# Last and first products by halves of the tokens, and local attention on stacked fp32r halves

## The chip, the cores and the metric

The kernel runs on one core of one Trainium2 chip. The metric is device time in microseconds (us) of one execution; the figure for a kernel is the median of several runs. A profile is of one execution. Engines are written as the profile writes them: PE is TensorE's matmuls, PEld its weight loads, DVE is VectorE, ACT is ScalarE, POOL is GpSimd and SP is SyncE, whose queue issues DMAs in this kernel (SPq).

## The reference

512 tokens of 1024 channels go through a first block and then through two layers of a second one, all in fp32. Cut to what matters:

```python
def first_block(x, mem, ...):
    z = rms_norm(x, norm_mix_g) @ w_in            # gating unit and sparse attention (nsa)
    x = x + mixed @ w_out
    x = x + memory_cross_attention(rms_norm(x, norm_mem_g), mem, ...)
    x = x + square(relu(rms_norm(x, norm_ffn_g) @ w_ff1)) @ w_ff2

def mod_norm(x, m, i, g):
    return rms_norm_2(x, g) * (1 + m[:, 3 * i + 1, None]) + m[:, 3 * i, None]
def ffn_sublayer(x, m, i, g, w1, w2):
    return x + HALF_STEP * m[:, 3 * i + 2, None] * swiglu(mod_norm(x, m, i, g), w1, w2)

for l in range(2):                                # second_block; xc: a context of 256 tokens
    m, mc = silu(c) @ w_mod[l] + b_mod[l], silu(c_ctx) @ w_mod[l] + b_mod[l]
    x, xc = ffn_sublayer(x, m, 0, ...), ffn_sublayer(xc, mc, 0, ...)
    u = mod_norm(x, m, 1, ...) @ w_in[l]          # kc, vc: keys and values of the context
    y = concat(conv_mixer(u), pool_mixer(u), neighbourhood_attention(u, kc, vc, rpb[l])) @ w_out[l]
    x = x + m[:, 5, None] * y                     # l == 0: the context has a mixer of its own and a second ffn
    x = ffn_sublayer(x, m, 2, ...)
return rms_norm_2(x, final_g)
```

In the neighbourhood attention 8 heads of 64 channels attend, in four blocks of 128 query tokens, to a band of 256 local keys (with a bias that also masks) and to 256 context keys.

## The kernel before, in words

Activations lie feature-major: a tile holds 128 channels on the partitions and the tokens along a row, so x is eight tiles of 128x512. To keep fp32 accuracy with the faster fp32r matmuls, every product is three: a weight w is split into wh and wl on arrival (ScalarE casts `whi`, VectorE subtracts for `wlo`, line L348), an activation into h and l, and the kernel adds wh·h, wh·l and wl·h (L377, L378, L380 in `gemm_fm`). Weights come in pieces of up to 1024 columns (`raw`), issued on SP; `get` takes the next piece in a written-out list, splits pieces that come after it, and gives VectorE one *tick*: a share of the products of the modulation (c @ w_mod, lines L582, with the weight tile `wm`).

The order of the work is that of the program: each engine runs its queue in order. Beside the main chain the kernel keeps a queue of other work (`fill`: the context's keys, values, mixer, the mixers' products), from which it takes a piece of some us at marked places.

A feed-forward sublayer goes by groups of hidden tiles (`GROUPS1`, `GROUPS2`): `up` makes a group, `dn` multiplies the group before into x (residual on VectorE). In the third and fourth feed-forward stage the 512 tokens of x and the 256 of the context go together: `gemm_fm` gets two outputs, `mm` of 512 columns and `aux` of 256, and takes them in turn for each k. PSUM has five banks for `mm`.

At a **seam** between two sublayers the last residuals end, the sums of squares go over the partitions by a product with ones (L468), give the reciprocal root (L436, L419), are spread over the partitions (L477), and `norm` makes for each k the h tile on ScalarE (L500) and the l tile on VectorE (L502), after a VectorE product with gain and root (L499). `norm_now` surrounds this with fills; the first two products of the next sublayer run k by k beside the norm (`gemm_fm_pair`, L391 to L408).

Local attention (`attend`) runs units (block j, head) through a pipeline: scores of unit i on PE (plain fp32, L1594 to L1599), bias and row maximum on VectorE (L1600 to L1603), the exponential on ScalarE in two halves (L1604, L1605); two units later four transposes (L1619) and a ScalarE copy (L1621), and two later P·V (L1636). Biases are loaded on SP (L1592) into three buffers. The first layer's stage lies at 1530 to 1660 us, the second's at 3000 to 3120, with other products (`fill`) between the units. The first block's sparse attention (200 to 460 us) is built alike, with transposed tiles copied by ScalarE (L1096) before P·V (L1110); `mem_kv` makes the memory's keys, squares them on ScalarE (L1160) and sums the squares with a product (L1164).

Of the kernel before, what the change touches and what calls it, by code (L numbers as in the profile page):

```python
# [16 lines left out]
T = 512  # L17
# [3 lines left out]
GROUPS2 = [4, 4, 4, 4, 4, 2]  # L21
GROUPS1 = [4] * 8
# [91 lines left out]
def lay_out(i):  # L114
# [44 lines left out]
    for s, j in enumerate((0, 1, 3)):  # L159
        key = np.arange(256) + BAND[j]  # L160
        if j == 1:
            key = np.concatenate([np.arange(256, 320), np.arange(64, 256)])
# [52 lines left out]

class Body:
    def __init__(self, ctx, tc, d, out, pk, at, order):
# [10 lines left out]
        self.used = []  # L228
# [107 lines left out]
    def ensure(self, i):  # L336
        order = self.order
        while len(self.split) <= min(i, len(order) - 1):
# [4 lines left out]
            hi = self.wp.tile([128, 1024], F32R, tag="whi", name="whi")[:, :nk * nc]  # L343
            lo = self.wp.tile([128, 1024], F32R, tag="wlo", name="wlo")[:, :nk * nc]
# [6 lines left out]
    def get(self, key, tick=1, ahead=2):  # L351
        i = len(self.used)
        self.used.append(key)
        if self.order is None:
            _, _, nk, nc = self.pk.pieces[key]
            w = [self.wp.tile([128, 1024], F32R, tag=t, name=t)[:, :nk * nc] for t in ("whi", "wlo")]
# [12 lines left out]
    def gemm_fm(self, outs, w, cols=slice(None), first=True, last=True):  # L369
# [137 lines left out]
    def norm_now(self, ready, *args):  # L507

        self.fill(FILL_A)
        it = self.norm(*args)  # L510
        next(it)
# [3 lines left out]
        if self.order:  # L515
            self.ensure(len(self.used) + 1)
        for _ in it:
            self.fill(FILL_B / 4)
# [103 lines left out]
    def pipeline(self, units, a, b, c, lag=2, lag_c=1, cost=2000):  # L622
# [381 lines left out]
    def nsa(self, qs, kh, kl, v2, gates, kc, vc, st_q, mh, ml):  # L1004
# [9 lines left out]
        P, PT, st = {}, {}, {}  # L1014
# [49 lines left out]
        def a(un):  # L1064
# [16 lines left out]
            nc.vector.tensor_scalar(m, m, r, -1.0, op0=OP.mult, op1=OP.mult)  # L1081
            P[un] = self.t2(w * n)
# [4 lines left out]
        def bb(un):  # L1087
# [8 lines left out]
            nc.scalar.copy(PT[un], t)  # L1096
# [42 lines left out]
        yield from self.pipeline(units, a, bb, cc, 3)  # L1139

    def mem_kv(self, mem, ss):
# [12 lines left out]
        st = self.b1.tile([128, 8], F32, name="mkst")  # L1154
        for h in range(4):
            p = self.mm()[:, :TC]
            self.gemm_fm([(p, hh, hl)], self.get(("mk", h)))
            nc.scalar.copy(self.mk[:, h], p)
            sq = self.t2(TC)
# [664 lines left out]
```

## Time and profile before

| | |
|---|---|
| median of 3 runs | 3551.36 us (3544.3 to 3551.93) |
| the profiled execution | 3549.73 us |
| its span | 3547.0 us |
| mean granted clock of TensorE | 0.979 |
| busy: PE, DVE, ACT, POOL | 97%, 57%, 34%, 3% |

The span is what the profiler saw of the program; the time has some 2.7 us more around it. The granted clock is a mean of two levels: 1 stands for 2.4 GHz, 0.5 for 1.2 GHz.

### The profile page before, as it was taken

To read this page: it belongs to the slowest core of one execution; us is meant where nothing else is said; L and a number is where in the kernel's file an instruction comes from. 1 tells how busy PE (TensorE), PEld (TensorE's weight loads), DVE (VectorE), ACT (ScalarE), POOL (GpSimd) and SP (SyncE) were. 2 spreads that over 40 slices of the span, in tenths; PEclk is the share of its full clock that TensorE was granted. 3 is DMA by queue.
4 is the path that set the end of the run, shared out by engine and by line. 5 is a ranking of instruction groups with operands and counts; after the bars stand their busy time and mean duration, and the time that the engine had idled before them with its cause. 6 is when DMAs were issued, how large, how long until landed. Compare 5 with 4: busy or idle time off the path is not lost.

```text
span 3547.0 us, 48466 instructions
## 1 busy us (share of the span) xinstructions
PE 3437.6 (97%) x18942; PEld 2966.9 (84%) x18942; DVE 2006.4 (57%) x4287; ACT 1209.6 (34%) x2519; POOL 110.8 (3%) x164
## 2 busy tenths in 40 slices
PE   8878999999999999999999999999999999999999
PEld 7868889788888888888888888888888888878887
DVE  5566657656776667655655555464444354554445
ACT  5445535533332223355422222132212134432222
POOL 1000000100000000000000000010000010000000
PEclk9988999999999999999999999999999999999999
DMA  4543334344444443432333333323233223223332
GB/s 168 172 124 118 94 123 142 123 149 143 145 140 143 145 149 120 144 118 88 96 96 93 96 98 91 94 72 95 90 98 95 78 66 117 61 64 106 100 97 78
DMA packets 140788, 392.60 MB, mean 111 GB/s; under 512 B 15632, under 2 KB 26768, under 8 KB 140048
## 3 DMA queue, kind: packets, MB, share of 16 engines
q1 hardware_dynamic: 92176, 301.42, 26.9%
q10 hardware_dynamic: 48384, 88.10, 8.5%
q8 instruction: 148, 2.42, 0.3%
q14 instruction: 80, 0.66, 0.1%
HBM read 387.36 MB, written 2.10 MB: 110 GB/s over the span
## 4 chain that ended last, share of the span: by engine, by line
PE 87%; DVE 6%; ACT 3%; issue 2%; DMA 1%; POOL 0%; SPq 0%; ACTq 0%; POOLq 0%; DVEq 0%
PE mm L377 20%; PE mm L380 20%; PE mm L378 20%; PE aux L377 5%; PE aux L378 5%; PE aux L380 5%; DVE wlo L348 2%; PE aux L1636 2%; PE mm L1619 1%; PE mm L406 1%; PE mm L407 1%; PE mm L408 1%; PE mm L391 1%; PE mm L392 1%; PE mm L396 1%
## 5 line engine op out<-in xcount | busy, mean ns | idle before, releaser
L348 DVE TENSOR_TENSOR wlo<-raw,whi 128x512 fp32r<-128x512 f32 (+1 forms) x1060 | 695.5, 698 | 455.9 <-ACT whi L347 449.3
L377 PE MATMUL mm<-h,whi 128*128 128x512 f32 (+1 forms) x2352 | 905.1, 385 | 11.5 <-ACT whi L347 11.5
L347 ACT CAST whi<-raw 128x512 fp32r<-128x512 f32 (+1 forms) x1060 | 599.4, 616 | 874.3 <-issue 726.5
L380 PE MATMUL mm<-h,wlo 128*128 128x512 f32 (+1 forms) x2352 | 896.8, 381 | 0.4 <-DVE wlo L348 0.4
L378 PE MATMUL mm<-h,whi 128*128 128x512 f32 (+1 forms) x2352 | 895.1, 381 | 0.3 <-DVE h L1002 0.3
L377 PEld LDWEIGHTS mm<-h,whi 128*128 128x128 f32 x2352 | 446.5, 190 | 105.5 <-ACT whi L347 11.7
L380 PEld LDWEIGHTS mm<-h,wlo 128*128 128x128 f32 x2352 | 447.6, 190 | 57.8 <-DVE wlo L348 1.1
L378 PEld LDWEIGHTS mm<-h,whi 128*128 128x128 f32 x2352 | 446.5, 190 | 56.1 <-issue 0.7
L377 PE MATMUL aux<-h,whi 128*128 128x256 f32 x1056 | 305.2, 289 | 3.3 <-DVE xc L1365 1.9
L378 PE MATMUL aux<-h,whi 128*128 128x256 f32 x1056 | 301.2, 285 | 0.5 <-DVE h L502 0.3
L380 PE MATMUL aux<-h,wlo 128*128 128x256 f32 x1056 | 300.2, 284 | 0.0
L377 PE MATMUL mm<-g,whi 128*128 128x512 f32 (+1 forms) x720 | 279.6, 388 | 0.0
L380 PE MATMUL mm<-g,wlo 128*128 128x512 f32 (+1 forms) x720 | 278.8, 387 | 0.0
L378 PE MATMUL mm<-g,whi 128*128 128x512 f32 (+1 forms) x720 | 277.8, 386 | 0.0
L582 DVE CUSTOM_DVE_ANT_0 wm<-wm,silu_c 128x512 f32<-128x512 f32 x336 | 231.2, 690 | 20.0 <-DMA wm<-in_wmod 13.9
L1411 DVE SCALAR_TENSOR_TENSOR t<-t,mm 128x512 f32<-128x512 f32 x88 | 60.5, 687 | 313.4 <-PE mm L380 312.8
L1365 DVE SCALAR_TENSOR_TENSOR x<-mm,gate,x 128x512 f32<-128x512 f32 x160 | 119.9, 749 | 207.2 <-PE mm L380 207.0
L411 ACT CAST g<-t 128x512 fp32r<-128x512 f32 x88 | 54.6, 621 | 526.1 <-DVE t L1411 526.1
L377 PEld LDWEIGHTS aux<-h,whi 128*128 128x128 f32 x1056 | 203.5, 193 | 35.9 <-DVE xc L1365 2.0
L378 PEld LDWEIGHTS aux<-h,whi 128*128 128x128 f32 x1056 | 203.1, 192 | 31.3 <-DVE h L502 1.3
L380 PEld LDWEIGHTS aux<-h,wlo 128*128 128x128 f32 x1056 | 204.5, 194 | 0.0
L377 PEld LDWEIGHTS mm<-g,whi 128*128 128x128 f32 x720 | 135.4, 188 | 28.1
(369 smaller groups left out, 4984.5 us busy)
## 6 DMA issues: line engine op xcount, KB each, us to landing
raw<-in_w_a SPq DMA_DIRECT2D x220, 512.0 KB, 3.5
wm<-in_wmod ACTq DMA_DIRECT2D x336, 256.0 KB, 2.7
raw<-in_w_d SPq DMA_DIRECT2D x110, 512.0 KB, 3.5
raw<-in_w_in SPq DMA_DIRECT2D x84, 512.0 KB, 3.6
raw<-in_w_f SPq DMA_DIRECT2D x64, 512.0 KB, 3.6
raw<-in_w_out SPq DMA_DIRECT2D x32, 512.0 KB, 3.5
bias<-in_bias SPq DMA_DIRECT2D x64, 128.0 KB, 2.2
fc<-in_cw SPq DMA_DIRECT2D x8, 512.0 KB, 4.5
```

Source lines behind the costliest of these rows:

```text
L347: self.nc.scalar.copy(hi[:, cs], raw[:, cs])
L348: self.nc.vector.tensor_tensor(lo[:, cs], raw[:, cs], hi[:, cs].bitcast(F32), op=OP.subtract)
L377: mmul(o, wh[:, k, cols], h[:, k], start=s, stop=False)
L378: mmul(o, wh[:, k, cols], l[:, k], start=False, stop=False)
L380: mmul(o, wl[:, k, cols], h[:, k], start=False, stop=e)
L391: mmul(o, wh[:, k], h[:, k], start=n == 0, stop=False)
L392: mmul(o, wl[:, k], h[:, k], start=False, stop=False)
L411: self.nc.scalar.copy(hi, src)
L582: nc.vector.tensor_tensor_reduce(o, w, self.sc[:, s, ks], 1.0, 0.0, OP.mult, OP.add, wm[:, half, s, j % 8:j % 8 + 1])
L1365: nc.vector.scalar_tensor_tensor(xs, o, gate[:, m:m + 1], xs, op0=OP.mult, op1=OP.add)
L1411: nc.vector.scalar_tensor_tensor(hid, hid, 0.5, b, op0=OP.mult, op1=OP.mult)
L1636: nc.tensor.matmul(o, PT[un][:, k * 128:(k + 1) * 128], v, start=k == 0, stop=k == len(vs) - 1)
```

## The change

`gemm_fm` takes the outputs one after the other. The last `dn` of each sublayer goes by halves of 256 tokens (`tail`), and so do the first two products of the next one (`gemm_halves`); the norm is made per half (`norm_half`), in steps that are issued between these products; `meet` keeps the fills that stood around the norm, ahead of the first products. The last pieces of a feed-forward's second weight are kept in SBUF for both halves (`kept`) and so are all fetched before the first half, in groups `GROUPS1` of 4 and 3 hidden tiles (nine in place of eight) and `GROUPS2` that ends on 3, 3. `mix_out` does its last three tiles by halves. The local attention takes the units by head, then block; scores are four fp32r products over a contraction of 128, made of stacked halves: q1 = [h; l], q2 = [l; h] and kk = [h; l] of one head, built one head ahead (`stack`), q2 by two DMAs from q1. The exponential is one operation of 512 columns and is issued one unit later (`e`); the row maximum is one over 512 columns, the second half of the bias buffer being zero; there are two bias buffers. In the sparse attention the exponential is one step later too, and copies of the first two blocks go to VectorE; in `mem_kv` the sums of squares go one step later.

```diff
-GROUPS2 = [4, 4, 4, 4, 4, 2]
-GROUPS1 = [4] * 8
+GROUPS2 = [4, 4, 4, 4, 3, 3]
+GROUPS1 = [4] * 5 + [3] * 4
+HALVES = (slice(0, 256), slice(256, T))
...
-        for k in range(nk):
-            s, e = first and k == 0, last and k == nk - 1
-            for o, h, l in outs:
+        for o, h, l in outs:
+            for k in range(nk):
+                s, e = first and k == 0, last and k == nk - 1
                 mmul(o, wh[:, k, cols], h[:, k], start=s, stop=False)
                 mmul(o, wh[:, k, cols], l[:, k], start=False, stop=False)
-            for o, h, l in outs:
                 mmul(o, wl[:, k, cols], h[:, k], start=False, stop=e)
...
+    def gemm_halves(self, jobs, hooks={}):
+        mmul = self.nc.tensor.matmul
+        hh, hl = self.h
+        n0, n1 = self.norms
+        for half, cs in enumerate(HALVES):
+            for n in range(9):
+                if half == 0:
+                    n0.to(4 + n)
+                    n1.to({2: 1, 6: 2, 8: 3}.get(n, 0))
+                else:
+                    n1.to(4 + n)
+                    if n in hooks:
+                        hooks[n]()
+                if n < 8:
+                    for o, (wh, wl) in jobs:
+                        mmul(o[:, cs], wh[:, n], hh[:, n, cs], start=n == 0, stop=False)
+                        mmul(o[:, cs], wl[:, n], hh[:, n, cs], start=False, stop=False)
+                if n:
+                    for o, (wh, wl) in jobs:
+                        mmul(o[:, cs], wh[:, n - 1], hl[:, n - 1, cs], start=False, stop=n == 8)
...
+    def norm_half(self, half, ss, g, sh):
+        nc = self.nc
+        cs = HALVES[half]
+        hh, hl = self.h
+        y = self.col_rstd(ss, 256, 1024)
+        yield
+        p = self.spread(y, 2)
+        yield
+        ts = {}
+        for k in range(9):
+            if k < 8:
+                ts[k] = self.t2(256)
+                nc.vector.scalar_tensor_tensor(ts[k], self.x[:, k, cs], g[:, k:k + 1], p[:, :256], op0=OP.mult,
+                                               op1=OP.mult)
+                nc.scalar.activation(hh[:, k, cs], ts[k], AF.Identity, bias=sh[:, k:k + 1])
+            if k:
+                nc.vector.scalar_tensor_tensor(hl[:, k - 1, cs], ts.pop(k - 1), sh[:, k - 1:k],
+                                               hh[:, k - 1, cs].bitcast(F32), op0=OP.add, op1=OP.subtract)
+            yield
...
+    def tail(self, ms, product, residual, ss, l, i, cost, each=None):
+        ss = [Squares(ss.sum[:, cs]) for cs in HALVES]
+        if l < 2:
+            gs, sh = self.mods(l, 0, i)
+            g = self.keep(8)
+            self.nc.vector.tensor_copy(g, gs)
+            self.h = self.new_h()
+            self.norms = [Steps(self.norm_half(h, ss[h], g, sh)) for h in range(2)]
+            steps = {8: (0, 1, 1, 1, 2, 3, 4, 5), 3: (1, 2, 4)}[len(ms)]
+        else:
+            self.ss = ss
+            self.norms = [Steps(self.norm_out())] * 2
+            steps = (0, 0, 1, 1, 1, 1, 2, 2)
+        for h, cs in enumerate(HALVES):
+            late = []
+            for n, m in enumerate(ms):
+                o = self.mm()[:, :256]
+                product(m, o, cs)
+                residual(m, o, cs)
+                self.sq_add(ss[h], self.x[:, m, cs], m, late)
+                if h:
+                    self.norms[0].to(steps[n])
+                if each:
+                    each(h, n)
+                yield cost
...
+            if e is not None and 0 <= i - 1 < n:
+                e(units[i - 1])
...
-            nc.scalar.copy(PT[un], t)
+            if b < 2:
+                nc.vector.tensor_copy(PT[un], t)
+            else:
+                nc.scalar.copy(PT[un], t)
...
+                if g == len(GROUPS1) - 1:
+                    ws = [self.get(("f2", g, m), 1, 3 - m, True) for m in range(4)]
+                    if self.order:
+                        self.ensure(len(self.used) + 1)
+                    def product(m, o, cs):
+                        self.gemm_fm([(o, gh[:, :, cs], gl[:, :, cs])], ws[m // 2], cols=slice(m % 2 * 128, m % 2 * 128 + 128))
+                    return self.run(self.tail(range(8), product, add, self.new_ss(T), 0, 0, 0))
...
+    def stack(self, hd, q_t, k_t):
+        nc = self.nc
+        t, i = hd // 2, hd % 2
+        q1, q2, kk = self.q1[i], self.q2[i], self.kk[i]
+        hs, os = slice(64 * i, 64 * i + 64), slice(64 - 64 * i, 128 - 64 * i)
+        def halves(o, x):
+            nc.scalar.copy(o[hs], x)
+            nc.vector.tensor_tensor(o[os], x, o[hs].bitcast(F32), op=OP.subtract)
+        halves(q1, q_t[hs, t])
+        nc.sync.dma_start(q2[os].bitcast(F32), q1[hs].bitcast(F32))
+        nc.sync.dma_start(q2[hs].bitcast(F32), q1[os].bitcast(F32))
+        yield
+        halves(kk[:, :T], k_t[hs, t])
+        yield
+        halves(kk[:, T:], self.kc[hs, t])
+        yield
+    def attend(self, q_t, k_t, v_t, vc, l, first, mixed, bias, tmp, tmp_t, rows, ready=lambda: True):
+        nc = self.nc
+        units = [(hd, j) for hd in range(8) for j in range(4)]
+        S, P, PT, cur = {}, {}, {}, {}
+        vcf = vc.rearrange("p k n -> p (k n)").rearrange("p (b n) -> p b n", b=2)
+        work = first
+        self.run(work)
+        def a(un):
+            nonlocal work
+            hd, j = un
+            i, b0 = hd % 2, BAND[j]
+            if j == 0 and hd < 7:
+                work = self.stack(hd + 1, q_t, k_t)
+            next(work, None)
+            p = self.mm()
+            if i == 0 and j == 0:
+                cur["s", hd // 2] = self.keep(8)
+            m, pr, bt = self.small(1), tmp(), bias[j % 2]
+            nc.sync.dma_start(bt[:, :256], self.d["bias"][l, (0, 1, 1, 2)[j], hd])
+            for o, ks in ((p[:, :256], slice(b0, b0 + 256)), (p[:, 256:], slice(T, T + TC))):
+                for n, q in enumerate((self.q1[i], self.q2[i])):
+                    nc.tensor.matmul(o, q[:, j * 128:(j + 1) * 128], self.kk[i][:, ks], start=n == 0, stop=n == 1)
+            nc.vector.tensor_tensor_reduce(pr, p, bt, -1.0, 3e38, OP.add, OP.min, m)
+            S[un] = pr, m
...
+        def e(un):
+            hd, j = un
+            n = 4 * (hd % 2) + j
+            P[un], m = S.pop(un)
+            nc.scalar.activation(P[un], P[un], AF.Exp, bias=m, scale=-1.0,
+                                 accum_out=cur["s", hd // 2][:, n:n + 1])
```

How the order of instructions moves at three places. On SP, in the second layer's attention, before (bias<-in_bias is one unit's bias; raw is a piece of weight of the fill):

```order
L1592 DMA bias<-in_bias 128x256 [waits DMAHW6_49,DVE_49]
L1592 DMA bias<-in_bias 128x256 [waits DMAHW7_49,DVE_49]
L1592 DMA bias<-in_bias 128x256 [waits DMAHW4_49,DMAHW0_49,DVE_49]
L332 DMA raw<-in_w_out 128x1024 [waits DVE_49]
L1592 DMA bias<-in_bias 128x256 [waits DMAHW2_49,DVE_49]
```

and now, one head of the same stage (q is the name of q1 and q2):

```order
L351 DMA raw<-in_w_in 128x1024
L1758 DMA q_26318<-q_26316 64x512 [waits DMAHW0_49,PE_49,Activation_49]
L1759 DMA q_26318<-q_26316 64x512 [waits DMAHW1_49,DVE_49]
L1788 DMA bias<-in_bias 128x256 [waits DMAHW5_49,DMAHW2_49]
L1788 DMA bias<-in_bias 128x256 [waits DMAHW6_49]
L1788 DMA bias<-in_bias 128x256 [waits DMAHW2_49,DVE_49]
L1788 DMA bias<-in_bias 128x256 [waits DMAHW3_49,DVE_49]
```

The two copies into q2 stand ahead of the bias of the head's first unit, and they wait for ScalarE and VectorE. On ScalarE in that stage now (`spare` is a unit's row of probabilities or its transpose, q_26314 the layer's q, k_26312 its k, fc the context's k):

```order
L1799 ACTIVATE spare,kp<-spare,sm 128x512 [waits DVE_49]
L1755 CAST q_26315<-q_26314 64x512
L1808 COPY spare<-mm 128x512 [waits PE_49]
L1799 ACTIVATE spare,kp<-spare,sm 128x512 [waits DVE_49]
L1755 CAST kk<-k_26312 64x512
L1808 COPY spare<-mm 128x512 [waits PE_49,Activation_49]
L1799 ACTIVATE spare,kp<-spare,sm 128x512 [waits DVE_49]
L1755 CAST kk<-fc 64x256
```

The cast of q for the next head stands behind the exponential of the unit before; before, no cast stood there. On VectorE, where the second block begins (x is normed for the first time), before:

```order
L499 SCALAR_TENSOR_TENSOR t_9429<-x,sm,aux 128x512 [waits DVE_49,PE_49]
L499 SCALAR_TENSOR_TENSOR t_9432<-x,sm,aux 128x512
L502 SCALAR_TENSOR_TENSOR h<-t_9429,mod,h 128x512 [waits Activation_49]
L348 TENSOR_TENSOR wlo<-raw,whi 128x512 [waits DMAHW7_49,Activation_49]
L348 TENSOR_TENSOR wlo<-raw,whi 128x512 [waits Activation_49]
L1365 SCALAR_TENSOR_TENSOR xc<-aux,gate,xc 128x256 [waits PE_49] x2
L499 SCALAR_TENSOR_TENSOR t_9472<-x,sm,aux 128x512
L502 SCALAR_TENSOR_TENSOR h<-t_9432,mod,h 128x512 [waits DVE_49]
L499 SCALAR_TENSOR_TENSOR t_9476<-x,sm,aux 128x512
```

and now, from the last of the splits and ticks that stand between the third and the fourth step of the first half's norm:

```order
L571 SCALAR_TENSOR_TENSOR h<-t_9546,mod,h 128x256 [waits Activation_49]
L370 TENSOR_TENSOR wlo<-raw,whi 128x512 [waits DMAHW3_49,Activation_49]
L370 TENSOR_TENSOR wlo<-raw,whi 128x512 [waits Activation_49]
L1483 SCALAR_TENSOR_TENSOR xc<-aux,gate,xc 128x256 [waits PE_49] x2
...
L672 ISA wj,modp<-wm,silu_c 128x512 [waits DMAHW3_49]
L672 ISA modp 128x1
L672 ISA wm,modp<-wm,silu_c 128x512 [waits DVE_49]
L672 ISA modp 128x1
L567 SCALAR_TENSOR_TENSOR t_9665<-x,kp,aux 128x256
L571 SCALAR_TENSOR_TENSOR h<-t_9564,mod,h 128x256
```

Six splits and two ticks (four products of wm) now stand between two steps of the norm, where two splits stood. In the same queue, ahead of the first half's residuals of that seam, stand eight splits and eight products of wm with no residual between them.

## Rows read from the trace of the kernel before

**Rows 1.** The page: busy time by engine, and the chain by engine.
```profile
PE 3437.6 (97%) x18942; PEld 2966.9 (84%) x18942; DVE 2006.4 (57%) x4287; ACT 1209.6 (34%) x2519; POOL 110.8 (3%) x164
...
PE 87%; DVE 6%; ACT 3%; issue 2%; DMA 1%; POOL 0%; SPq 0%; ACTq 0%; POOLq 0%; DVEq 0%
```

**Rows 2.** Windows: length, busy by engine, PEclk, DMA; last: sum of five seams.
```profile
1000.00:1030.00 30.00, 28.72 (x164) 25.15 (x163) 25.25 (x47) 13.38 (x22) 1.39 (x1) 0.94 0.34 105
...
2310.00:2345.00 35.00, 27.87 (x147) 24.39 (x147) 27.04 (x55) 16.14 (x30) 6.82 (x9) 0.85 0.15 46
...
3000.00:3120.00 120.00, 118.89 (x708) 98.00 (x708) 60.25 (x173) 60.82 (x175) 0.14 (x2) 1.00 0.20 61
...
sum 180.00, PE 155.28 PEld 135.61 DVE 129.37 ACT 79.99 POOL 24.86; mean PE 31.06 PEld 27.12 DVE 25.87 ACT 16.00 POOL 4.97
```

**Rows 3.** Waits, whole span: who waited for whom, us, times, longest.
```profile
PE aux L1110 <- ACT t L1096: 19.6, 10, 4.6
...
PE mm L391 <- ACT h L500: 12.8, 5, 4.0
```

**Rows 4.** Timeline of PE at 1004 us: one output after the other.
```profile
1004.01 0.39 PE L380 MATMUL mm<-gh,wlo 128*128 128x512 f32 x1
...
1004.69 0.39 PE L380 MATMUL mm<-gh,wlo 128*128 128x512 f32 x1
...
1005.15 0.28 PE L380 MATMUL aux<-fc,wlo 128*128 128x256 f32 x1
...
1007.67 0.28 PE L380 MATMUL aux<-fc,wlo 128*128 128x256 f32 x1
```

**Rows 5.** Timeline of PE at 2000 us: outputs in turn, first and ninth.
```profile
2000.08 0.28 PE L380 MATMUL aux<-fc,wlo 128*128 128x256 f32 x1
...
2008.51 0.28 PE L380 MATMUL aux<-fc,wlo 128*128 128x256 f32 x1
```

**Rows 6.** VectorE groups by line: busy and mean ns, or ns min/median/max.
```profile
L348 DVE TENSOR_TENSOR wlo<-raw,whi 128x512 fp32r<-128x512 f32 (+1 forms) x1060 | 695.5, 698 | 455.9 <-ACT whi L347 449.3
...
L582 DVE CUSTOM_DVE_ANT_0 wm<-wm,silu_c 128x512 f32<-128x512 f32 x336 | 231.2, 690 | 20.0 <-DMA wm<-in_wmod 13.9
...
L499 DVE SCALAR_TENSOR_TENSOR t<-xc,kp,aux x40: 468/474/481, 231.2 to 2953.3; 128x256 f32<-128x256 f32 x40
```

**Rows 7.** Chain in the second layer's attention: start us, us, what.
```profile
3005.88 0.44 PE mm L1619 x4
...
3007.15 0.63 PE mm L1594 x2
...
3008.21 0.59 PE mm L1619 x4
...
3010.69 0.59 PE mm L1619 x4
...
3022.20 0.44 PE mm L1619 x4
```

**Rows 8.** ScalarE, ns min/median/max: exponential, its sum, copy, cast.
```profile
L1604 ACT ACTIVATE spare<-spare,sm x32: 507/508/511, 2990.8 to 3114.7; 128x256 f32<-128x256 f32 x32
L1604 ACT ACTIVATION_READ_ACCUMULATOR spare<-spare,sm x32: 185/187/190, 2991.3 to 3115.1; 128x1 f32 x32
...
L1621 ACT COPY spare<-mm x32: 570/572/644, 2998.6 to 3116.3; 128x512 f32<-128x512 f32 x32
...
L818 ACT CAST kh<-uv x4: 614/618/621, 76.3 to 82.4; 64x512 fp32r<-64x512 f32 x4
```

**Rows 9.** SP: bias landing (page), its waits 1530 to 1660, one issue.
```profile
bias<-in_bias SPq DMA_DIRECT2D x64, 128.0 KB, 2.2
...
SPq L1592 <- DVE sm L1601: 49.6, 23, 3.2
...
3027.75 0.33 SPq L1592 DMA_DIRECT2D bias<-in_bias  x1
```

**Rows 10.** Waits of PE from 165 to 200 us.
```profile
PE aux L1164 <- ACT t L1160: 7.4, 2, 5.7
```

More of the change, by code (lines that the diff above doesn't have):

```diff
@@ L1154, in mem_kv, with stat @@
         st = self.b1.tile([128, 8], F32, name="mkst")
+        y = self.b1.tile([128, 8], F32, name="mky")
+        todo = []
+        def stat(h, sq):
+            a = self.mm()
+            for b in range(2):
+                nc.tensor.matmul(a[:, b:b + 1], sq[:, b * 128:(b + 1) * 128], self.c("ones"), start=True, stop=True)
+            nc.vector.tensor_copy(st[:, h:8:4], a[:, :2])
+            if h == 3:
+                self.head_rstd(st, pair, 128, y, True)
         for h in range(4):
@@ L1648, in cc, with stacks @@
                 self.after(1, scale)
-                def out():
-                    if ready():
-                        self.run(self.to_fm(O, None, 4, j, None, *mixed()))
-                    else:
-                        self.after(2, out)
+                self.after(2, lambda: self.run(self.to_fm(O, None, 4, j, None, *mixed())))
+        yield from self.pipeline(units, a, bb, cc, 2, 2, 1400)
+        self.flush()
+    def stacks(self, pool):
+        self.q1 = [pool.tile([128, T], F32R, tag=f"q1{i}", name="q1") for i in range(2)]
+        self.q2 = [pool.tile([128, T], F32R, tag=f"q2{i}", name="q2") for i in range(2)]
+        self.kk = [pool.tile([128, T + TC], F32R, tag=f"kk{i}", name="kk") for i in range(2)]
@@ L1655, in cc, with mix_out, residual, product @@
                 self.after(2, out)
-        yield from self.pipeline(units, a, bb, cc, *(((2, 2) if l == 0 else (2, 2)) if k_t is not None else (2,2, 1400)))
+        yield from self.pipeline(units, a, bb, cc, 2, 2, e=e)
         self.flush()
-    def mix_out(self, l, s, n, x, ss, mh, ml):
+    def mix_out(self, l, x, mh, ml):
         nc = self.nc
-        gate = self.gate(l, s, 1)
-        late = None if s else []
-        for m in range(8):
-            p = self.mm()[:, :n]
-            self.gemm_fm([(p, mh, ml)], self.get((("o", l), m), s == 0))
-            nc.vector.scalar_tensor_tensor(x[:, m], p, gate[:, m:m + 1], x[:, m], op0=OP.mult, op1=OP.add)
-            self.sq_add(ss, x[:, m], m, late)
-            if s == 0:
-                self.fill(FILL_OUT)
-            yield n * 10
+        gate = self.gate(l, 0, 1)
+        ss, late = self.new_ss(T), []
+        def residual(m, o, cs):
+            nc.vector.scalar_tensor_tensor(x[:, m, cs], o, gate[:, m:m + 1], x[:, m, cs], op0=OP.mult, op1=OP.add)
+        for m in range(5):
+            p = self.mm()
+            self.gemm_fm([(p, mh, ml)], self.get((("o", l), m)))
+            residual(m, p, slice(0, T))
+            self.sq_add(ss, x[:, m], m, late)
+            self.fill(FILL_OUT)
+        while late:
+            late.pop()()
+        ws = {m: self.get((("o", l), m), 1, 7 - m) for m in range(5, 8)}
+        def product(m, o, cs):
+            self.gemm_fm([(o, mh[:, :, cs], ml[:, :, cs])], ws[m])
+        def each(h, n):
+            if h and self.order:
+                self.ensure(len(self.used) + n)
+            self.fill(FILL_OUT / 2)
+        self.run(self.tail(range(5, 8), product, residual, ss, l, 2, 0, each))
@@ L1690, in mix2 @@
                     if l:
[L1691 removed]
+                        self.attend_spread(q_t, k_t, v_t, first, bias, work)
                         att = ()
@@ L1769, in block2 @@
                     norm_c = self.norm_c(l, 2 * f, False) if both else None
-                    work = self.ffn2(l, f, True, both, norm_c, end if (l, f) == (1, 1) else None)
+                    work = self.ffn2(l, f, True, both, norm_c)
                     for c in work:
```

295 lines of the change are left out of this document (162 added, 133 removed).

## Prediction

> **What bounds the kernel now.** I read the page's busy line and the chain first: TensorE is busy for 97% of the span, and 87% of the chain that ended last is its matmuls, with VectorE's split of a weight a distant second [rows 1]. The reader is to see that a saving of matmul time counts almost in full where nothing else is late. So I looked for the stretches in which TensorE is not the last: the windows. In the second layer's local attention it is busy for 118.9 of 120 us at full clock [rows 2]: that stage is bound by TensorE alone. At the seams between sublayers it is not: in the five seams from the end of the third feed-forward stage to the last one it idles 180 − 155.3 = 24.7 us, and in the worst the mean clock is 0.85 [rows 2]. The waits say what ends last there: the first products wait for the first normed tile, 12.8 us in five times; in the sparse attention of the first block the P·V product waits for a ScalarE copy, 19.6 us in ten [rows 3].
>
> **The change, part by part.** The sum is made against the profiled execution, 3549.7 us (its span of 3547.0 and 2.7 around it); the median of the runs is 1.6 us above that.
>
> *Products of two streams in another order.* `gemm_fm` ran a 512-column and a 256-column product in turn over each k; now all k of one stream come first, then the other. Alone, a triple (wh·h, wh·l, wl·h) takes 0.68 us at 512 columns (1004.01 to 1004.69) and 0.36 at 256 (seven in 2.52 us) [rows 4]; in turn eight pairs of triples take 8.43 us, 1.054 each [rows 5]. 1.054 − 1.04 = 0.014 us, times 1056 pairs (as many as the second stream has triples) is **−14.6 us**; bounds 0 and −20.
>
> *Halves of the tokens.* The counts of the order say that 744 products of 512 columns become 1488 of 256. 2 × 0.120 − 0.227 = 0.013 us each [rows 4]: **+9.7 us**; bounds 0 (the halves at half the time) and +15.
> The Trainium skill's "TensorE: Matmul & The Clock Gate", section "Back-to-back issue gap", gives 518 cycles at 512 columns and 262 at 256 at the full clock; by it the split would cost only 744 × 6 cycles, about 2 us, and the sum would be 8 us lower. The rows show 11 ns over both of its figures, so I keep the rows.
>
> *The seams.* Gone is the wait of the first product for a norm that began after the last residual: the norm of the first half now runs while the second half's products do. Of the 24.7 us of idle time the 12.8 us above are that wait [rows 3]. TensorE's clock is half for a while behind such waits: at 2310 to 2345 the mean is 0.85, so 2 × 0.15 × 35 = 10.5 us at 1.2 GHz behind waits that add up to 7.1 us [rows 2]; of that cost, some 20 us in the five seams, I let 8 go. Against it stands VectorE: one k of a half norm is two operations of 0.474 us [rows 6], 0.95 us, where TensorE needs only 6 × 0.12 = 0.72 us for it, so it catches up with the norm by 8 × 0.23 = 1.8 us per half, and the splits of the next weights are queued ahead of later norm steps; I charge 1.2 us per seam: −12.8 − 8 + 6 = **−15 us**, bounds −25 (all idle time) and 0.
>
> *The seam from the first block's feed-forward to the second block.* There TensorE lost little before (1.3 us idle, clock 0.94) [rows 2]. Now all four last pieces of the weight are fetched at once, and each fetch puts its splits and a modulation tick into VectorE's queue before the first half's residual: eight splits (four of 512 columns at 0.698, four of 256 at half that), 4.2 us, and eight products of 0.690 us with a read behind each, 5.5 us or more [rows 6], about 10 us. TensorE has five PSUM banks for half products of 9 × 0.12 = 1.08 us: 5.4 us of work, then it waits some 5. Then four splits to six and four ticks, some 7 us, stand between the third and fourth norm step, where VectorE's queue before had the norm steps in a row; this costs 4 to 5 more. With the clock behind it: **+12 us**; bounds 0 (ticks hidden under the group before) and +18.
>
> *Local attention.* TensorE's work per unit falls: the scores were plain fp32 products, 1.06 us (3007.15 to 3008.21); now four fp32r products of 256 columns, 0.48 us. That is −0.58 × 64 = −37 us if nothing else became late. But the rest does. A unit was 2.48 us from transposition to transposition [rows 7]. Now the exponential of a unit stands on ScalarE behind the copy of the one before, and the transposition needs it: exp → four transposes → copy → next exp. The exp over 512 columns is between the copy of 512 (0.57) and two of 256 (1.02) [rows 8]; I take 0.75, as the copy's growth suggests, with 0.19 for the sum; with 0.44 for the transposes and 0.57 for the copy, and some 0.2 for hand-overs, the loop is 2.15 us. Four units without anything else would gain 4 × 0.33 = 1.3 us.
> At unit j = 0 of heads 0 to 6 (14 in both layers), `stack` for the next head adds a ScalarE cast, 0.62 us, which stands behind the exp of the unit before [rows 8]; a VectorE subtraction (not in the trace at this place; the 128x512 one is 0.698 [rows 6]); and two DMAs q2 ← q1 on SP that wait for both. The unit's own bias load is queued on SP **behind** these. SP waits in order: before, the bias issues stood 49.6 us behind VectorE's row maximum in the first attention stage, which hurt nobody since three buffers were in use [rows 9]; now there are two, and the head's first bias can't be early. From the end of the preceding exp: cast 0.6, subtraction 0.7, two issues and the bias's own, 0.33 each [rows 9], landing 2.2 us later [rows 9], masked add with the minimum over 512 columns (0.474 for an operation of 256 columns, 0.698 for one of 512 [rows 6]; 0.75 taken), exp 0.94: the transposition starts after some 6 us where the loop would have it after 2.15. So TensorE waits about 3.8 us per head. The kk casts and subtractions of the next two units stand ahead of their masked adds: 1 us more. A head is then 8.6 + 3.8 + 1.1 = 13.5 us without other work. In the second layer four units took 16.3 us before (3005.88 to 3022.20) [rows 7], 6.4 more than four times 2.48: other products behind the fourth unit. They stand away from the wait; I let 1.6 of them be hidden: 13.5 + 4.8 = 18.3, **+2 per head**, +14. In the first layer other work comes every third unit, and part of it lands in the wait; I take a third of that, +4. The clock behind waits of 3.8 us: by the seam above up to 2.6 us each, but TensorE isn't last in these loops, so +6 for 14. Together **+24 us**; bounds −27 (no late bias) and +54 (the clock in full).
>
> *Sparse attention of the first block.* The exponential goes one step later, and half the copies go to VectorE: of the 19.6 us of waits [rows 3] I take a third, **−6**; bounds −20 and +5. *Statistics of the memory's keys* go a step later: of 7.4 us of waits for the square [rows 10], **−4**; bounds −7 and 0.
>
> Sum: −14.6 + 9.7 − 15 + 12 + 24 − 6 − 4 = +6.1, so 3555.8 for the profiled execution, 3557 us beside the median.
>
> **The rivals.**
> 1. *The first bias of a head isn't late, or nobody feels it*, and the attention stages go by the 2.15 us loop: −27 in place of +24, **3506 us**. For it: TensorE has two units of work queued ahead, and SP waited for 49.6 us before without harm [rows 9]. Against it: that work is 1.75 us a unit (1.27 from the transposes to the scores [rows 7], and 0.48), and the wait of 3.8 us is what is left behind it.
> 2. *Slower: the clock.* If each of the 14 late biases leaves TensorE at 1.2 GHz as the waits at 2310 to 2345 did, 5 us at half clock each [rows 2], and this falls on the other products (6.4 us behind the fourth unit), each costs 2.6: 14 × 2.6 = 36 in place of 6, **3587 us**. [...]
> 3. *The fetches at the first seam are spread by the copies' own waits*, so that VectorE's burst is hidden: 0 in place of +12, **3545 us**. For it: VectorE is busy for only 57% [rows 1]. Against: its queue is in order, and the burst stands before the residual.
> 4. *The 256-column products cost nothing more*, since the 0.120 us belongs to the stretch of the row and not to the shape: 0 in place of +9.7, **3547 us**. For it: nothing but that one stretch was read. Against: 24 products in a row have that spacing [rows 4]. This is nearly what the two figures of the Trainium skill's page, named above, would give.
>
> **How the numbers follow.** Some 0.2%, 7 us, is about what a measurement of this kernel can tell from no change: 3544 to 3558. The forecast gets 0.42, with its own range of 3538 to 3578 from half of the bounds of its terms (0.05 faster, 0.16 same, 0.21 slower). Rival 1 gets 0.27, all faster. Rival 2 gets 0.18, all slower. Rival 3 gets 0.08 (0.02 faster, 0.06 same), rival 4 0.05, same. Together: faster 0.34, same 0.27, slower 0.39. The range of 3505 to 3590 leaves out half of rival 1 and a third of rival 2, 0.19.
>
> **What would show it.** Right: in the attention stages a wait of the masked add for the bias DMA at the first unit of each head, SP waiting for ScalarE or VectorE ahead of it, 18 us per head in the second layer, TensorE's share there below 85%; at the first seam a wait of TensorE for VectorE's residual behind a row of ticks; the first products of the other seams waiting for a few us in all in place of 12.8. In the stages of both streams the pair of triples at 1.04 us. Wrong: attention units 2.2 us apart across heads (rival 1), a mean clock under 0.85 in the attention windows (rival 2), no gap at the first seam (rival 3), or half-width triples at 0.34 us (rival 4). If the sum of terms is right and the time isn't, I expect the fault in the attention term, which has the widest bounds.

## The result, and the profile after

The changed kernel takes 3597.7 us (3596.4 to 3599.8, four runs) beside 3549.6 us for the kernel before (the median of four runs by now): ratio 1.0142, 95% interval 1.0129 to 1.0155. It is 48 us slower; 3557 was forecast, with a range up to 3590.

The page of the changed kernel, its busy line and its chain, answers to [rows 1]:

```profile
PE 3416.5 (95%) x19618; PEld 3016.3 (84%) x19618; DVE 2065.8 (57%) x4426; ACT 1241.7 (35%) x2537; POOL 112.7 (3%) x178
...
PE 84%; DVE 8%; ACT 4%; DMA 3%; issue 2%; SPq 0%; ACTq 0%; POOL 0%; DVEq 0%; POOLq 0%
```

TensorE is busy for 21 us less and the program is 49 us longer; DMA, 1% of the chain before, has 3%. The windows of the two local-attention stages, and one head of the second (answering to [rows 2]):

```profile
1527.00:1673.00 146.00, 122.90 (x877) 116.17 (x875) 78.54 (x175) 76.97 (x166) 0.14 (x2) 0.91 0.33 100
3020.00:3176.00 156.00, 126.27 (x728) 112.66 (x727) 68.48 (x142) 69.97 (x146) 0.14 (x2) 0.87 0.23 71
3036.00:3056.00 20.00, 16.12 (x91) 14.21 (x90) 9.93 (x21) 9.55 (x19) 0.00 (x0) 0.83 0.21 66
```

In the kernel before, the same two stages are

```profile
1522.00:1659.00 137.00, 135.43 (x922) 117.59 (x920) 77.11 (x225) 74.08 (x212) 0.14 (x2) 1.00 0.30 93
2990.00:3126.00 136.00, 134.78 (x778) 109.93 (x777) 66.34 (x191) 67.39 (x192) 0.14 (x2) 1.00 0.22 68
```

TensorE was busy there for 99% at full clock; now it is for 84% and 81%, at mean clocks of 0.91 and 0.87. Its waits over the whole span, the longest first (answering to [rows 3]; L1806 is the transposes, L1799 the exponential, L439 and L443 the first products by halves, L569 and L571 the h and l tiles of the norm, L1396 and L1494 residuals):

```profile
PE mm L1806 <- ACT spare L1799: 28.3, 12, 3.9
PE mm L1806 <- ACT p L1799: 19.0, 12, 3.9
PE mm L439 <- ACT h L569: 15.5, 4, 5.5
PE mm L443 <- DVE h L571: 12.1, 2, 6.1
...
PE mm L402 <- DVE x L1396: 7.9, 1, 7.9
PE mm L402 <- DVE x L1494: 6.4, 3, 2.3
```

The wait for the first h tile, 12.8 us before, is gone but for 1.8 us at the last seam. But the products of the first half now wait in their middle, for the third or fourth h tile: 2.7, 5.5 and 5.4 us ahead of feed-forward 0,0, of layer 0's mixers and of feed-forward 0,1 (1005, 1394 and 1780 us), 13.6 in all, where the first tile took 0.9, 2.4 and 0 before. Ahead of feed-forward 1,0 and of layer 1's mixers, where it took 3.9 and 4.0, no h tile is waited for. The wait for an l tile, 12.1 us in two times, is new.

Where the time went shows when the traces are cut into stages. Each cut is the start of one instruction that all kernels have (the first square of the first block's feed-forward; the first and last product with tanh of a feed-forward stage; the first masked add and the first output residual of a mixer). Lengths in us, by profile:

| stage | before | changed | halves_alone | attention_alone | block1_and_order |
|---|---|---|---|---|---|
| first block up to its feed-forward | 674.7 | 649.3 | 670.3 | 671.7 | 651.5 |
| its feed-forward, first seam | 358.5 | 369.4 | 370.1 | 358.5 | 358.5 |
| feed-forward 0,0 | 311.1 | 312.3 | 312.3 | 311.1 | 311.1 |
| seam, mixers of layer 0 | 178.1 | 196.2 | 191.6 | 183.4 | 178.9 |
| local attention of layer 0 | 137.0 | 145.9 | 136.6 | 145.8 | 137.0 |
| output product, seam | 114.3 | 128.7 | 126.3 | 113.9 | 114.7 |
| feed-forward 0,1 (both streams) | 494.1 | 491.9 | 497.6 | 494.1 | 488.0 |
| seam | 78.0 | 78.6 | 79.2 | 77.5 | 78.6 |
| feed-forward 1,0 (both streams) | 494.1 | 491.7 | 497.6 | 494.2 | 488.1 |
| seam, mixers of layer 1 | 150.0 | 156.4 | 153.3 | 152.7 | 150.8 |
| local attention of layer 1 | 136.0 | 155.7 | 134.8 | 157.2 | 136.0 |
| output product, seam | 60.6 | 59.3 | 59.6 | 59.6 | 60.5 |
| feed-forward 1,1 | 311.3 | 310.9 | 310.9 | 311.3 | 311.3 |
| end | 49.2 | 49.8 | 49.8 | 49.2 | 49.2 |

The last three columns are runs told of below: one part of the change each, on the kernel before.

### The profile page after: what moved, and what is told of

It is laid out like the page before. It is cut to its first block, busy times and chain, and to the rows that moved or that the text cites. A ratio compares the mean times of both kernels' runs of the same rounds, so it can differ in the third digit from the quotient of the medians.

```text
span 3596.1 us, 50089 instructions
## 1 busy us (share of the span) xinstructions
PE 3416.5 (95%) x19618; PEld 3016.3 (84%) x19618; DVE 2065.8 (57%) x4426; ACT 1241.7 (35%) x2537; POOL 112.7 (3%) x178
## 4 chain that ended last, share of the span: by engine, by line
PE 84%; DVE 8%; ACT 4%; DMA 3%; issue 2%; SPq 0%; ACTq 0%; POOL 0%; DVEq 0%; POOLq 0%
PE mm L402 19%; PE mm L403 19%; PE mm L404 19%; PE aux L402 5%; PE aux L404 5%; PE aux L403 5%; DVE wlo L370 2%; DMA wm<-in_wmod 1%; PE aux L1820 1%; PE mm L453 1%; PE mm L454 1%; PE mm L455 1%; DMA bias<-in_bias 1%; PE mm L1806 1%; PE aux L1213 1%
## 5 line engine op out<-in xcount | busy, mean ns | idle before, releaser
L370 DVE TENSOR_TENSOR wlo<-raw,whi 128x512 fp32r<-128x512 f32 (+2 forms) x1088 | 697.7, 683 | 455.0 <-ACT whi L369 446.8
L369 ACT CAST whi<-raw 128x512 fp32r<-128x512 f32 (+2 forms) x1088 | 603.4, 605 | 936.9 <-issue 708.0
L402 PEld LDWEIGHTS mm<-h,whi 128*128 128x128 f32 x2400 | 458.6, 191 | 93.1 <-ACT whi L369 11.9
L404 PEld LDWEIGHTS mm<-h,wlo 128*128 128x128 f32 x2400 | 457.4, 191 | 82.4 <-DVE wlo L370 0.7
L403 PEld LDWEIGHTS mm<-h,whi 128*128 128x128 f32 x2400 | 458.4, 191 | 76.9 <-issue 0.7
L402 PE MATMUL mm<-g,whi 128*128 128x512 f32 (+1 forms) x800 | 293.6, 367 | 6.4 <-DVE x L1494 6.4
L403 PE MATMUL mm<-g,whi 128*128 128x512 f32 (+1 forms) x800 | 292.5, 366 | 0.0
L404 PE MATMUL mm<-g,wlo 128*128 128x512 f32 (+1 forms) x800 | 291.5, 364 | 0.0
L402 PEld LDWEIGHTS mm<-g,whi 128*128 128x128 f32 x800 | 152.0, 190 | 28.7 <-DVE x L1494 7.0
L404 PEld LDWEIGHTS mm<-g,wlo 128*128 128x128 f32 x800 | 151.7, 190 | 24.4
```

What stands on the lines that cost most here:

```text
L369: self.nc.scalar.copy(hi[:, cs], raw[:, cs])
L370: self.nc.vector.tensor_tensor(lo[:, cs], raw[:, cs], hi[:, cs].bitcast(F32), op=OP.subtract)
```

## The experiments

Times are medians, each beside the kernel before on the same chip (3543.6 to 3546.1 us). The changed kernel was timed beside one of 3549.6, so a difference from its 3597.7 us can be 4 to 6 us too large; where it is small, the profiles and their stages say more.

**bias_first.** In `attend`, the bias load goes ahead of the stack step:

```diff
+            m, pr, bt = self.small(1), tmp(), bias[j % 2]
+            nc.sync.dma_start(bt[:, :256], self.d["bias"][l, (0, 1, 1, 2)[j], hd])
             next(work, None)
             p = self.mm()
...
-            m, pr, bt = self.small(1), tmp(), bias[j % 2]
-            nc.sync.dma_start(bt[:, :256], self.d["bias"][l, (0, 1, 1, 2)[j], hd])
```

> The changed kernel, with each unit's bias load issued on SP ahead of the stack step, so ahead of the two copies into q2. Theory (the head's first bias is late since SP waits for ScalarE and VectorE first): the waits of the transposes of 3.7 to 3.9 us at the first unit of each head go, and the half clock of 6.8 us behind them; 14 x 3.8 less what the kk casts leave (1 us a head stays) and with 1 to 2 us of clock back per head: 35 to 50 us less than the changed kernel, so 3548 to 3563 us. Rival (the added casts and subtractions and the loop of exponential, transposes and copy make the head long, whatever the bias does): under 10 us less, 3588 to 3598 us.

3556.8 us: 41 less than the changed kernel. What it undoes is seen in the changed kernel's chain of waits at the head of 3036 us (start, length, what):

```profile
3033.59 0.71 ACT spare L1799 x2
3034.30 0.51 ACT q L1755
3034.81 0.02 issue
3034.84 0.70 DVE q L1756
3035.55 0.47 SPq L1759
...
3036.11 2.29 DMA bias<-in_bias
...
3038.53 0.69 DVE spare L1792
...
3039.27 0.82 ACT spare L1799 x2
...
3040.13 1.12 PE mm L1806 x4
3041.25 1.60 PE aux L1820 x8
```

Exponential, cast of q, subtraction, copy into q2, bias, masked add, exponential: one after the other, 5.8 us from the end of one exponential to the transposes. The products behind run at half clock (granted clock 0.50 from 3041.25 to 3044.66 us): the eight of P·V take 1.60 us, 0.83 before (from the end of the first transposes to the scores, 3006.32 to 3007.15) [rows 7]. With the bias ahead, the windows of the two stages of bias_first are:

```profile
1527.00:1655.00 128.00, 117.08 (x887) 110.12 (x888) 78.56 (x176) 77.53 (x167) 0.14 (x2) 0.97 0.38 117
2995.00:3131.00 136.00, 117.72 (x744) 102.89 (x743) 68.65 (x143) 70.99 (x148) 0.14 (x2) 0.97 0.28 84
```

128 and 136 us for 146 and 156; and on SP the copy still waits, but the head's bias no longer stands behind it (waits of bias_first, 2995 to 3131 us):

```profile
SPq L1758 <- ACT q L1755: 48.5, 6, 9.2
```

So it was the place in the queue, not the casts. In the first layer 128 us are 9 less than before; in the second, 136 us are what the stage took before. A third bias buffer, which the kernel before had, was not tried.

**ctx_norm_after** and **steps_then_ctx_norm.** In the two stages of both streams, the rest of the context's norm is a hook at step 6 of the second half. First it was moved behind `gemm_halves`, then left at its place with x's last norm steps ahead of it:

```diff
-    hooks = {2: lambda: next(norm_c), 6: lambda: self.run(norm_c)}
+    hooks = {2: lambda: next(norm_c)}                                # ctx_norm_after: run(norm_c) after gemm_halves
+    hooks = {2: lambda: next(norm_c), 6: lambda: (self.norms[1].to(12), self.run(norm_c))}   # steps_then_ctx_norm
```

> The changed kernel, with the rest of the context's norm issued after the first products' halves and not before their last steps (two seams, ahead of the third and fourth feed-forward stage). Theory (VectorE does eight k of the context's norm before the last l tile of x): the two waits of 6.0 us ahead of the last wh x l products go, and the half clock behind them; the context's first product then waits a part of it, for its own norm: 8 to 16 us less than the changed kernel, 3582 to 3590 us. Rival (the time only moves to the context's first products, whose norm is as long wherever it stands): within 4 us, 3594 to 3602 us.

> The changed kernel, with the last norm steps of the second half issued just ahead of the context's norm, at the same place of the program. Theory (the two waits of 6.0 us are VectorE's queue: eight k of the context's norm ahead of the last l tile): both waits go, and with them the half clock behind, and the context's products find their norm as early as before: 12 to 18 us less than the changed kernel, 3580 to 3586 us, more than ctx_norm_after gave. Rival (VectorE is simply full there, whatever the order): no more than ctx_norm_after, 3588 us and over.

3590.3 us (7 less) and 3587.6 us (10 less): under what was expected both times, and with ratios (1.0130, 1.0117 to 1.0144, and 1.0123, 1.0106 to 1.0141) whose intervals overlap that of the changed kernel, so the medians alone show no gain. The profiles do. In the second kernel the waits of L443 are gone from the list, and of 12 us of waits and what the clock adds some 11 come back (3596.1 to 3584.7). In both kernels each stage of both streams takes 488.0 us, as in block1_and_order, where it was 491.9 and 491.7. The changed kernel's chain shows the place (L546 to L549 are the context's norm, L571 the last l tile of x):

```profile
1793.01 0.49 DVE t L546
...
1799.52 0.48 DVE h L549
1800.01 0.41 DVE h L571
1800.46 0.80 PE mm L443 x2
```

**ticks_after.** The ticks of the fetches at the seams go elsewhere (those of the first two weights behind the halves; those of the kept weights into the group before; those of the last output weights into the second half):

```diff
-        self.gemm_halves([(p, self.get((("k", l), m), 1, 2 - m)) for m, p in enumerate(ps)])
+        self.gemm_halves([(p, self.get((("k", l), m), 0, 2 - m)) for m, p in enumerate(ps)])
+        self.tick(2)
...
-                    w = self.get(("f2", g, mp_))
+                    w = self.get(("f2", g, mp_), 2 if g == len(GROUPS1) - 2 else 1)
```

> The changed kernel, with the modulation ticks of the fetches at the seams moved: those of the first products' two weights to behind their halves, those of the first feed-forward's kept weights into the group before, those of the last three output weights into the second half. Theory (VectorE's ticks stand ahead of the norm steps and residuals, and some of them wait for their own DMA): the waits of 5.5, 5.4 and 2.7 us for the first h tile and of 7.9 us for the residual at the first seam shrink to less than half, 10 to 18 us less than the changed kernel, 3580 to 3588 us. Rival (the splits of the weights, which stay, make the wait): under 5 us less, 3593 to 3598 us.

3582.2 us: 15 less, 14 by the profiles. The waits for h tiles, which the expectation calls those for the first, fall from 15.5 to 6.7 us (2.7, 5.5 and 5.4 at the three seams become 0, 2.3 and 2.5), the longest wait for the residual at the first seam from 7.9 to 3.4. In the changed kernel VectorE's timeline at the second seam was, ahead of the norm's fourth step (L567):

```profile
1388.29 1.82 DVE L370 TENSOR_TENSOR wlo<-raw,whi 128x512 fp32r<-128x512 f32 x2 [0.77 <-ACT whi L369]
1390.04 0.68 DVE L672 CUSTOM_DVE_ANT_0 wj<-wm,silu_c 128x512 bf16<-128x512 f32 x1
1390.65 0.08 DVE L672 DVE_READ_ACCUMULATOR2_ANT modp<- 128x1 f32 x1
1390.76 0.69 DVE L672 CUSTOM_DVE_ANT_0 wm<-wm,silu_c 128x512 f32<-128x512 f32 x1
1391.38 0.08 DVE L672 DVE_READ_ACCUMULATOR2_ANT modp<- 128x1 f32 x1
1391.85 0.69 DVE L672 CUSTOM_DVE_ANT_0 wj<-wm,silu_c 128x512 bf16<-128x512 f32 x1 [0.40 <-DMA wm<-in_wmod]
...
1393.20 0.48 DVE L567 SCALAR_TENSOR_TENSOR t<-x,kp,aux 128x256 f32<-128x256 f32 x1
```

and on TensorE, which had begun the half at 1385.54 us with the first three h tiles, the first product of the fourth waited for it from 1388.78 us on:

```profile
1394.28 0.58 PE L439 MATMUL mm<-h,whi 128*128 128x256 f32 x1 [5.50 <-ACT h L569]
```

The seam after that has the same burst, two splits and four products of wm up to the norm's step:

```profile
1774.78 1.48 DVE L370 TENSOR_TENSOR wlo<-raw,whi 128x512 fp32r<-128x512 f32 x2 [1.05 <-ACT whi L369]
...
1779.38 0.47 DVE L567 SCALAR_TENSOR_TENSOR t<-x,kp,aux 128x256 f32<-128x256 f32 x1
```

And ahead of a residual of layer 0's output product (L1855) a tick waits for the landing of its own weight, in the changed kernel's chain:

```profile
1710.62 4.96 DMA wm<-in_wmod
...
1715.60 0.69 DVE wj L672
...
1717.32 0.40 DVE x L1855
```

**three_fixes** has bias_first, ctx_norm_after and ticks_after together; **one_split_less** also splits one piece less ahead of the halves (`ahead` of the two fetches one lower).

> The changed kernel with the three edits before together: bias ahead of the stack step, context's norm behind the halves, ticks moved. If the three causes are separate, as they lie at different places, their gains add: 41 + 7 + 15 less than 3598, so 3530 to 3540 us, faster than the kernel before. Rival (they share one wait, for instance VectorE as a whole being short of time): less than two thirds of the sum, over 3555 us.

> As three_fixes, with the piece after the first products' two weights split behind the halves, not ahead of them (one piece: two casts on ScalarE and two subtractions on VectorE). Theory (the splits of the next weights in VectorE's queue are what is left of the wait of the first h tile at the seams): 1.4 to 1.8 us of VectorE at each of five seams, and some clock: 4 to 12 us less than three_fixes. Rival (those splits are hidden by products that don't need the norm, or the wait goes to the next product, whose weight is late): within 3 us of three_fixes, or longer.

3537.9 us, 60 less than the changed kernel where the sum of the three was 63 (59 and 63 by the profiles): the gains add, as those of separate causes do. It is faster than the kernel before (0.9974, 0.9961 to 0.9988). With one split less it is 3551.4, 13 more where 4 to 12 less were expected: feed-forward 0,0 goes from 310.9 to 318.1 us, with a wait of 4.9 for a weight's cast that three_fixes does not have there, and the two with both streams go from 488.0 to 492.6 and 490.9. The splits ahead of the halves are not free (without that one layer 0's output product and seam take 119.3 us for 123.9), but without them a later weight is late.

**order_alone.** The kernel before with `gemm_fm` in the new order, as in the diff.

> The kernel before with the new order of gemm_fm alone. The prediction's term: 14.6 us less than before (3535 us). Rival (what the stages of the changed kernel show, 2 to 3 us less in each of the two long ones): 5 to 8 us less, 3541 to 3545 us.

3535.1 us: 0.9975 (0.9966 to 0.9984), 8.6 us less by the medians, 13.7 by the two profiles. Its timeline at 2000 us:

```profile
2000.28 0.28 PE L379 MATMUL aux<-fc,wlo 128*128 128x256 f32 x1
...
2001.36 0.28 PE L379 MATMUL aux<-fc,wlo 128*128 128x256 f32 x1
...
2001.95 0.39 PE L379 MATMUL mm<-g,wlo 128*128 128x512 f32 x1
...
2002.64 0.39 PE L379 MATMUL mm<-g,wlo 128*128 128x512 f32 x1
...
2003.32 0.39 PE L379 MATMUL mm<-g,wlo 128*128 128x512 f32 x1
```

Three triples of 256 columns take 1.08 us, and one of 512 takes 0.69 and the next 0.68: a pair takes 1.05 just behind the change of shape and 1.04 after it, for 1.054 in turn. The two long stages give 5.8 and 6.1 us [rows 4, 5].

**sparse_alone** and **block1_and_order.** The first is the kernel before with the sparse attention's edits of the diff alone; the second has `mem_kv`'s and `gemm_fm`'s order as well.

> The kernel before with the sparse attention's part of the change alone (exponential one step later, copies of the first two blocks on VectorE), without mem_kv's. The first block took 674.7 us before and 649.3 in the changed kernel. Theory (ScalarE's exponential, standing ahead of the copies of older steps while it waits for VectorE's maximum, held up P V): most of it, 15 to 25 us less than before, 3520 to 3530 us. Rival (the prediction's size): 6 us less, and mem_kv the rest.

> The kernel before with three parts of the change that moved no work to the seams: the sparse attention's, mem_kv's, and gemm_fm's order. By the stages of the changed kernel the first block gives 25 us and by order_alone the order 9 to 13 us; they lie in different stages, so 3505 to 3512 us, faster than before by 1.0% and more. Rival (the first block's gain came from the other parts, as less work waits in the queue of fills): 3525 us and over.

3526.0 us, 19 less (0.9945, 0.9932 to 0.9959), and 3515.8 us, 29 less (0.9909, 0.9893 to 0.9925), 4 over the range expected. TensorE's waits for the P·V product from 200 to 460 us in sparse_alone (L1107 and L1109 are the copies on VectorE and ScalarE):

```profile
PE aux L1123 <- DVE t L1107: 6.3, 3, 4.8
...
PE aux L1123 <- ACT t L1109: 2.6, 5, 0.6
```

19.6 us of waits for ScalarE's copy became 2.6 and 6.3. The 2.6 are in the last two blocks, whose copies stayed on ScalarE and whose exponential alone moved (10.0 before, from 295 us on); in the first two, whose copies went to VectorE, two other products (L1104, L1076) now wait for these copies too, 3.9 and 3.5 us. The first block up to its feed-forward goes from 674.7 to 652.4 us, and `mem_kv` adds 0.9 at most: of the 6.4 us of waits for the square that sparse_alone still has from 160 to 200 us, none is left in block1_and_order, but products wait there for 5.7 us in its place, 3.6 of them for a weight's cast.

**attention_alone** and **best_with_attention.** The kernel before with the diff's local attention; and block1_and_order with it and the bias ahead of the stack step.

> The kernel before with the change's local attention alone (stacked fp32r scores, units by head, one exponential a unit later, two bias buffers, bias behind the stack step). The prediction's term: 24 us more than before, 3569 us; by the stages of the changed kernel 28 us and some products that moved out of the stages, up to 3585 us. Rival (the count of matmul time): 37 us less, 3508 us.

> block1_and_order with the new local attention too, its bias issued ahead of the stack step. Theory (with the bias early the loop of exponential, transposes and copy and the casts of the stack make a head about as long as TensorE's work did before): within 10 us of block1_and_order, 3506 to 3526 us. Rival (with the bias early the count of matmul time comes in): 25 us less or more, 3490 us.

3582.3 us, 36 more than before; 3510.0 us, 36 less than before (0.9897, 0.9882 to 0.9913) and 6 less than block1_and_order, with intervals that overlap. The same attention, then, costs 36 us with its bias late and is worth a few us at most without: by the two profiles its stage in layer 0 gives 9 us and that in layer 1 none. best_with_attention has the lowest median of all kernels run.

**halves_alone.** The kernel before with the halves alone; every other part as before.

> The kernel before with the halves alone (tail, norm_half, gemm_halves, meet, the kept last pieces and the new groups), with the order of gemm_fm, the local attention, the sparse attention and mem_kv as before. The prediction's terms for this part: 9.7 - 15 + 12, 7 us more than before, 3553 us. Theory from the other runs, by subtraction (the changed kernel less attention_alone and less block1_and_order, stage by stage): 45 to 50 us more than before, 3590 to 3597 us, of it 11 at the first seam, 12 and 14 ahead of the two mixers' ends, 4 in each of the two stages with the context. Rival (the parts make each other worse, as when the late attention leaves work for the seams): 20 us or less more, under 3566 us.

3592.3 us, 48 more than before (1.0131, 1.0114 to 1.0148). The stages of the table above give 11.6 us at the first seam, 13.5 and 12.0 around layer 0's mixers, and 3.5 in each stage of both streams. The waits of L439's and L443's counterparts are those of the changed kernel:

```profile
PE mm L442 <- ACT h L572: 15.3, 5, 5.0
PE mm L446 <- DVE h L574: 12.1, 2, 6.1
...
PE mm L404 <- DVE x L1379: 7.9, 1, 7.9
```

The three parts add up to 48 + 36 − 29 = 55 us by the medians and 43 + 33 − 33 = 43 by the profiles, around the 48 of the whole change.

## Why the prediction was wrong

**The step that failed is the charge at the seams**: "the splits of the next weights are queued ahead of later norm steps; I charge 1.2 us per seam", in a term of −15 us. With 9.7 for the splits and 12 for the first seam, the halves were to cost 7 us; alone they cost 48, 41 more. That the whole is off by 41 too is chance: of the other terms, attention was 12 us too small and sparse attention's gain 13 too small, and these two cancel.

What the term was to remove did go: the wait of the first product fell from 12.8 us to 1.8. Others came in its place, inside the halves. In VectorE's queue the next weights' splits and ticks now stand between the steps of the first half's norm, 5 us of them at 1388 us, and a tick stands until its own DMA has landed (VectorE idles for 0.4 us there, and for 3.7 at 1712 us). I had read that order and priced it at the first seam (+12, measured +11 to 12; the wait for the residual was 7.9, that for the norm 2.7), and not at the next two, where the changed kernel's rows at 1388 and 1775 us show a burst of the same kind and TensorE waits for 5.5 and 5.4. At the two later seams no split and no tick stands between the steps, and there is no such wait. A second cause was in the code of the hooks and I had not seen it: the whole of the context's norm ahead of x's last l tile, twice 6.0 us. ticks_after (15 us) and steps_then_ctx_norm (7 to 11) show both. Together they are about half of the 48; the cause of the rest stays open.

**Local attention: the mechanism was right, the term of 24 too small**: 36 alone. The wait was put at 3.8 us per head: in the second layer it is 3.7 to 3.9 at six heads, in the first 3.9 once and 1.1 to 3.1 elsewhere. The head was put at 18.3 us, it takes 20.3 (3036.11 to 3056.44 from bias to bias). The likely difference is rival 2, to which I gave part of its price: TensorE is at half clock for a while behind each wait (a mean of 0.83 in the head above), and the other products run there; no run has the wait without the clock. Of the 33 us by profile 8 lie ahead of the two attention stages (183.4 and 152.7 us in the table, for 178.1 and 150.0); I had no term for them and no run shows why. Rival 1 is refuted; what it claimed, a gain of 27 us with an early bias, is refuted too: best_with_attention gains 6. Nor do the 27 follow from my loop: 64 units at 0.33 us are 21.

**The new order**: 14.6 forecast, 13.7 by profile, 11.9 in the two long stages and 8.6 by medians: right in the mechanism, somewhat large in size. **Sparse attention**: 6 forecast, a third of the waits; 19 measured. Where copies stayed on ScalarE the waits are nearly gone, since the exponential that waited for VectorE's maximum no longer stands ahead of older copies; the copies on VectorE show no such gain. The two edits were not run apart. **mem_kv**: 4 forecast, under 1 measured.

**The split into 256 columns**, +9.7, was not isolated; halves_alone has TensorE busy for 11.8 us more than before, half clock included. Rival 4 finds no support: the halves' own products stand 0.12 us apart in the changed kernel (1738.04, 1738.16, 1738.28 us). Contiguous 256-column products stand 0.120 us apart in order_alone as they did before, 11 ns over the figure for an isolated product (262 cycles) of the Trainium skill's "TensorE: Matmul & The Clock Gate", section "Back-to-back issue gap". Feed-forward 1,1 and the end, where halves meet no other late work, are within 1 us of before. Rival 3, no cost at the first seam, is refuted by the 11.6 us there in halves_alone.

What stays open: three_fixes is 28 us over best_with_attention (34 by the profiles), so with ticks and context norm moved the halves still cost that much, 9 and 10 us of it around layer 0's mixers, 6 at the first seam and 6 at the one ahead of feed-forward 1,0 (by the stages of the two profiles). What is seen there are waits of some 2 us for residuals and h tiles, of up to 2.8 us of the context's products for its norm, and one of 4.6 us in the context's attention (L1717); which of them must stay with halves was not tried.

## What to carry to other kernels

Before a step is cut finer so that it starts earlier, write down what stands in the slowest engine's queue between its first and last piece: splits, ticks and a neighbour's norm that were harmless behind the step are a wait when they are between its pieces. Price a burst at every place where the order shows it, not at the first. On a queue that issues DMAs, a load that could go at once belongs ahead of a copy that waits for two engines: that alone was some 41 of 3598 us here.

## What the runs showed of the hardware

In the second layer's attention TensorE waits once in each of six heads for 3.7 to 3.9 us. Behind such a wait its granted clock is 0.50, that is 1.2 GHz (3041.25 to 3044.66 us); the mean is 0.83 over a head and 0.87 over the stage. In bias_first the waits for the exponential in that stage are under 2 us, but for one of 3.1, and the mean is 0.97.

Products of 256 columns stand 0.120 us apart and those of 512 some 0.227, whichever of the two shapes a stretch has; in turn a pair of triples takes 1.054 us, one shape after the other 1.04 (order_alone).
